# Hybrid decoder layer on one core: warm products at the start, keys copied by transfers, a sink column, and the gated output weights prepared two units earlier

## The chip, the core and the metric

The kernel runs on one core of a Trainium2 chip. A core has a matrix engine (TensorE), VectorE, ScalarE and POOL (GpSimd) for elementwise work, and SyncE (SP), whose queue issues the transfers. Every engine takes its instructions in a fixed order, from its own queue. The metric is the device time of one execution in microseconds (us). In the rows, PE is TensorE, PEld its weight load, DVE VectorE, ACT ScalarE.

## The reference, cut to what matters

One decoder layer over 2048 tokens of width 1024: a modulated norm, one input projection, two groups of heads beside each other, an output projection whose result is gated, and a final norm.

```python
mod = jnp.dot(jax.nn.silu(c), w_ada) + b_ada
shift, scale, gate = jnp.split(mod, 3, axis=-1)
h = rmsnorm(x, g_norm) * (1.0 + scale) + shift
proj = jnp.einsum('bsd,de->bse', h, w_in)
gq, gk, gv, ga, gz, sq, sk, sv, sz = split_cols(proj, COL_SIZES)
z = jnp.einsum('bsr,rk->bsk', ga, w_decay) + b_decay
o_gla = gla_chunked(gq, gk, gv, log_sigmoid(z) / 16)      # 4 heads, chunks of 64
o_gla = rmsnorm(o_gla, g_gla_head) * silu(gz)
q, k = rope(sq, positions), rope(sk, positions)           # 8 query heads, 2 key heads of 64
# window of 128; one sink logit for each head joins the softmax and is dropped after it
probs = softmax(concat([scores, sink], -1))[..., :-1]
o_swa = einsum(probs, sv) * silu(sz)
y = jnp.einsum('bse,ed->bsd', concat([o_gla, o_swa]), w_out)
x = rmsnorm(x + gate * y, g_final)
```

Everything is float32. A product that has to be exact enough is made from two parts of each operand, a rounded high part and the rest (`h` and `l` in names), with three products: high x high, low x high, high x low.

## The kernel before

The tokens are worked through in four units of 512. In each, the norm's result (`hh`, `hl`, eight pairs of tiles) is multiplied with the input weights slot by slot: `qk`, `gz`, `sz`, `gv` and `sq` twice each, `kv` once. A slot's weights are fetched into one of two buffers (`wp`); the first unit splits them and keeps the parts in memory (`wc`), the others fetch them from there. `proj_t` gives products `pt`, `proj_n` gives `pn`. In between come the heads: `gla` (one call for a pair of heads; on VectorE its chain goes from `de` through the scans `bc`, `dd` and `qk` to the transposes `pk` on TensorE), and `swa_tile` (queries transposed into `pq`, split into `qs`; scores `psc`; the softmax in `s`; `ppt`, `ppo`). `k_rows` transposes a unit's keys into `pkr` and puts their parts into `kst`, for each of two key heads a high and a low tile, in which both halves of the 128 partitions hold the same 64 rows; `pq` and `pkr` share one buffer of the matrix engine's memory (tag `pqk`). `norm(u + 1)` prepares the next unit. After the last unit, 16 calls of `out_tile` multiply the mixed heads (`mixd`) with the output weights `wo` (products `py`).

At the start, `norm0_start` sums the squares of the first unit with products `ss`, `silu_rows` spreads the conditioning vector with products `pb`, and `warm` adds products `pw` whose result nobody reads. `proj_t_outer` then makes the first six products (`po`) while their weights (`wr_first`) and the modulation (`wa`) arrive.

`late_rows` computes the gate (`wg` loads, `gate` steps on VectorE, products `pg`), multiplies each block of `w_out` with it (`wor`), and splits it. It is called in the fourth unit. The first four blocks of each half stay on the chip; the other four are written to memory (`woc`) and fetched by `last_rows`.

The order of the instructions on every engine is no plain program order. Each call is recorded with its reads and writes, and `Order.issue` simulates the engines with a table of costs and lays down the order in which the recorded calls become ready there; among calls that are ready on an engine, the one with the lowest number goes first. `od.lift` is added to that number: -LIFT (600) moves a call forward, LATER (400) back. `od.together()` keeps calls side by side. In a trace all these instructions have the lines of three helpers (L377, L424, L429), so they are told apart by their tiles.

Of the kernel before, what the change touches and what calls it, by code (L numbers as in the profile page):

```python
# [8 lines left out]
F32 = mybir.dt.float32  # L9
# [47 lines left out]
LATE_AT = 'sz0'  # L57
WO_EARLY, WO_LATE = (0, 1, 2, 3), (4, 5, 6, 7)
WARM = 13
# [323 lines left out]
def layer_kernel(ctx, tc, x, xT, w_ada, w_gate, b_cols, b_gate, g_cols, c_cols, pos, inv_freq,  # L383
# [48 lines left out]
    def warm(n, after):  # L432

        p = att.tile([P, P], F32, name="pw", tag="pqk")
        for _ in range(n):
            mmul(p, ones, ident, True, True).deps.add(after)
# [21 lines left out]
    def load_small():  # L458
# [4 lines left out]
        nsk = const.tile([P, 8], F32, name="nsk")  # L463
        V.tensor_scalar(nsk, sk, -1.0, None, op0=ALU.mult)
        return gh, sk, nsk
# [93 lines left out]
    def late_rows():  # L559

        for i in range(2):
            sl = slice(i * NB, (i + 1) * NB)
            acc = keep.tile([P, NB], F32, name=f"gate{i}", tag="r1")
            for k in range(KT):
                wg = stp.tile([P, NB], F32, name=f"wg{i}{k}", tag="xs", bufs=2)
                SY.dma_start(wg, w_gate[:, k, sl])
                if k == 0:
                    V.tensor_scalar(acc, wg, s_c[:, 0:1], None, op0=ALU.mult)
                else:
                    V.scalar_tensor_tensor(acc, wg, s_c[:, k:k + 1], acc,  # L570
                                           op0=ALU.mult, op1=ALU.add)
            parts = [stp.tile([P, NB], F32R, name=f"ga{i}{j}", tag="xs", bufs=2) for j in range(2)]
            A.copy(parts[0], acc)
            V.tensor_tensor(parts[1], acc, f(parts[0]), ALU.subtract)
            pg = att.tile([P, NB], F32, name=f"pg{i}", tag="px")
            for j in range(2):
                mmul(pg, ones_r, parts[j], j == 0, j == 1)
            bg = stp.tile([P, NB], F32, name=f"bg{i}", tag="xs", bufs=2)
            SY.dma_start(bg, b_gate[:, sl].broadcast_to([P, NB]))
            V.tensor_tensor(acc, pg, bg, ALU.add)  # L580
            for k in range(KT):
                raw = stp.tile([P, NB], F32, name=f"wor{k}{i}", tag="st")
                SY.dma_start(raw, w_out[k * P:(k + 1) * P, sl])
                V.tensor_tensor(raw, raw, acc, ALU.mult)
                if k in WO_EARLY:
                    h_ = hp.tile([P, NB], F32R, name=f"woh{k}{i}", tag="hh")
                    l_ = hp.tile([P, NB], F32R, name=f"wol{k}{i}", tag="hl")
                else:
                    h_, l_ = [stp.tile([P, NB], F32R, name=f"wo{j}{k}{i}", tag="st") for j in "xy"]
                wo[k, i] = h_, l_  # L590
                A.copy(h_, raw)
                V.tensor_tensor(l_, raw, f(h_), ALU.subtract)
                if k not in WO_EARLY:
                    for j in range(2):
                        SY.dma_start(f(woc[:, j, k, sl]), f(wo[k, i][j]))

    def last_rows():

        for k in WO_LATE:
            for i in range(2):  # L600
                wo[k, i] = [hp.tile([P, NB], F32R, name=f"wo{j}{k}{i}", tag=f"h{j}") for j in "hl"]
                for j in range(2):
                    SY.dma_start(f(wo[k, i][j]), f(woc[:, j, k, i * NB:(i + 1) * NB]))
        for i in range(2):
# [103 lines left out]
    def rsqrt(r, ms):  # L708
# [684 lines left out]
```

## Time and profile before

| | |
|---|---|
| three timed runs | 873.10, 873.64, 873.64 us; median 873.64 |
| the profiled execution | 872.5 us, span 870.8 us |
| busy in the span | TensorE 97%, weight loads 84%, VectorE 66%, ScalarE 54%, POOL 43% |
| mean granted TensorE clock | 0.994 |
| transfers | 179.9 MB, mean 207 GB/s |

The span goes from the first to the last instruction. The granted clock is the share of 2.4 GHz that TensorE was given in a stretch; its two levels are 1.2 and 2.4 GHz. An engine's idle time matters where another engine waits for it.

### The profile page before, as it was taken

What the parts mean: (1) busy time and instruction counts of PE and PEld (TensorE: products, weight loads), DVE (VectorE), ACT (ScalarE), POOL (GpSimd) and SP (SyncE); (2) the same over time, 40 slices, a digit from 0 to 9 for tenths busy, and PEclk for the clock granted to TensorE, in tenths of its full rate; (3) what the DMA queues carried; (4) which work ended last, traced back from release to release, by engine and by line L of the source; (5) the groups of instructions that cost most, each with busy time, mean ns of one, the idle gap of its engine ahead of it and who ended that gap; (6) DMA issues with size and microseconds to landing.
All of it is one profiled execution on the core that took longest, in us unless ns stands there. A gap on an engine that the chain in (4) does not pass through costs nothing. (4 is left out here: it accounts for less than half of the span.)

```text
span 870.8 us, 14663 instructions
## 1 busy us (share of the span) xinstructions
PE 841.4 (97%) x5122; PEld 732.0 (84%) x5122; DVE 578.7 (66%) x1132; ACT 470.8 (54%) x1178; POOL 374.6 (43%) x436
## 2 busy tenths in 40 slices
PE   6999989999999999999999999998999999999997
PEld 4788979789898887898897989887879888888886
DVE  4997699877575577767447786877766654444442
ACT  3677657686464577646536655464386633333332
POOL 2621346658446345744425565244337242222221
PEclk9999999999999999999999999999999999999999
DMA  8969996774443466545337564759474864444421
GB/s 340 324 255 329 352 358 227 275 276 142 152 182 116 154 238 227 204 130 195 124 116 260 191 221 162 256 204 345 147 260 158 302 193 146 145 145 145 146 73 48
DMA packets 76000, 179.90 MB, mean 207 GB/s; under 512 B 8420, under 2 KB 24855, under 8 KB 72727
## 3 DMA queue, kind: packets, MB, share of 16 engines
q1 hardware_dynamic: 74918, 178.93, 58.5%
q8 instruction: 40, 0.66, 0.3%
q14 instruction: 34, 0.27, 0.1%
q10 hardware_dynamic: 1008, 0.05, 0.1%
HBM read 134.78 MB, written 44.17 MB: 206 GB/s over the span
## 5 line engine op out<-in xcount | busy, mean ns | idle before, releaser
L424 PE MATMUL py<-woh,m 128*128 128x512 f32 (+2 forms) x528 | 160.7, 385 | 0.1
L424 PEld LDWEIGHTS py<-woh,m 128*128 128x128 f32 x528 | 98.4, 188 | 20.1 <-DVE r L377 0.5
L424 PE MATMUL py<-wol,m 128*128 128x512 f32 (+2 forms) x264 | 101.4, 384 | 0.0
L377 POOL TENSOR_TENSOR r<-r,gf 128x512 f32<-128x512 f32 x31 | 45.8, 1480 | 114.6 <-ACT xr L377 111.9
L377 ACT ACTIVATE ge<-ge 128x512 f32<-128x512 f32 x96 | 60.6, 631 | 37.4 <-DVE ge L377 36.2
L424 PE MATMUL pn<-wh_gv,hh 128*128 128x272 f32 (+1 forms) x256 | 73.7, 288 | 0.0
L424 PE MATMUL pn<-wl_sq,hh 128*128 128x256 f32 x256 | 73.5, 288 | 0.2 <-DMA wl_sq<-wc 0.2
L424 PE MATMUL pn<-wh_sq,hl 128*128 128x256 f32 x256 | 73.4, 287 | 0.0
L424 PE MATMUL pn<-wh_gv,hl 128*128 128x272 f32 (+1 forms) x256 | 73.3, 287 | 0.0
L424 PE MATMUL pn<-wl_gv,hh 128*128 128x272 f32 (+1 forms) x256 | 73.3, 287 | 0.0
L424 PE MATMUL pn<-wh_sq,hh 128*128 128x256 f32 x256 | 72.7, 286 | 0.0
L377 DVE TENSOR_TENSOR r<-py,xr 128x512 f32<-128x512 f32 (+2 forms) x33 | 22.3, 675 | 62.5 <-PE py L424 62.5
L377 ACT ACTIVATE s<-s,nm 128x128 f32<-128x128 f32 x128 | 50.1, 393 | 20.7 <-DVE nm L377 20.5
L424 PEld LDWEIGHTS py<-wol,m 128*128 128x128 f32 x264 | 49.6, 188 | 9.7
L377 POOL TENSOR_TENSOR s<-s,den 128x512 f32<-128x512 f32 x32 | 35.6, 1111 | 43.7 <-DVE den L377 31.8
L377 POOL TENSOR_TENSOR xt<-xt,rstd 128x512 f32<-128x512 f32 x27 | 38.0, 1411 | 37.2 <-ACT rstd L377 15.6
L424 PEld LDWEIGHTS pn<-wl_sq,hh 128*128 128x128 f32 x256 | 49.4, 193 | 1.5 <-DMA wl_sq<-wc 0.4
L377 POOL TENSOR_TENSOR qr<-qr,rope 128x256 f32<-128x256 f32 x32 | 27.0, 863 | 54.1 <-DVE rope L377 54.1
L424 PEld LDWEIGHTS pn<-wh_sq,hl 128*128 128x128 f32 x256 | 49.3, 193 | 1.0 <-issue 0.3
L424 PEld LDWEIGHTS pn<-wh_sq,hh 128*128 128x128 f32 x256 | 49.2, 193 | 0.8 <-issue 0.2
L424 PEld LDWEIGHTS pn<-wh_gv,hh 128*128 128x128 f32 x256 | 48.4, 189 | 0.6
L424 PEld LDWEIGHTS pn<-wl_gv,hh 128*128 128x128 f32 x256 | 48.4, 189 | 0.5
(262 smaller groups left out, 2515.9 us busy)
## 6 DMA issues: line engine op xcount, KB each, us to landing
xr<-in_x SPq DMA_DIRECT2D x32, 256.0 KB, 2.8
mr<-mixd SPq DMA_DIRECT2D x16, 512.0 KB, 4.0
out<-r SPq DMA_DIRECT2D x32, 256.0 KB, 2.3
wa<-in_w_ada SPq DMA_DIRECT2D x7, 1024.0 KB, 7.7
xn<-in_x SPq DMA_DIRECT2D x24, 256.0 KB, 4.9
xt<-in_xT SPq DMA_DIRECT2D x24, 256.0 KB, 4.5
wl_sz<-wc SPq DMA_DIRECT2D x12, 512.0 KB, 5.8
wh_sz<-wc SPq DMA_DIRECT2D x12, 512.0 KB, 6.2
```

What stands on the lines that cost most here:

```text
L377: return order.add(eng, lambda: real(*args, **kw), dur, ins, outs, lock=lock, nbytes=nbytes)
L424: return od.add("PE", lambda: T.matmul(o, l, r, start=start, stop=stop), dur, [l, r] + ([] if start else [o]), [bank if start and bank is ...
```

## The change

- `warm(WARM0, None)` puts 14 products `pw` of 128 columns ahead of everything else on TensorE; nothing reads them.
- `k_rows` writes one half of each `kst` tile (ScalarE for the high part, VectorE for the low), straight from `pkr`, and SP copies it to the other half by a transfer: four for each unit. The copy `kt`, two POOL casts and two VectorE subtractions go.
- The sink becomes a 129th column of the scores (`s1`): it takes part in the maximum, the exponential and its sum. The separate exponential `es`, its addition and `nsk` go.
- The last steps of `rsqrt`, and the sums before it in `norm`, go from VectorE to POOL (three norms).
- `late_rows` becomes `out_weights(i)`, for one half of the output columns: the first is called after slot `sq1` of the second unit, the second after `sq1` of the third, with LATER. All eight blocks of a half pass through the ring of three `st` buffers and are written to `woc`; `out_fetch` brings the first four back in the fourth unit.
- The two products of a score tile's head stay side by side.

```diff
+OUT_AT = {1: ('sq1', 0), 2: ('sq1', 1)}
-LATE_AT = 'sz0'
+WARM0, WARM = 14, 13
...
-        V.tensor_tensor(t, r, r, ALU.mult)
-        V.tensor_tensor(t, t, ms, ALU.mult)
-        V.tensor_scalar(t, t, -0.5, 1.5, op0=ALU.mult, op1=ALU.add)
-        V.tensor_tensor(r, r, t, ALU.mult)
+        G.tensor_tensor(t, r, r, ALU.mult)
+        G.tensor_tensor(t, t, ms, ALU.mult)
+        G.tensor_scalar(t, t, -0.5, 1.5, op0=ALU.mult, op1=ALU.add)
+        G.tensor_tensor(r, r, t, ALU.mult)
...
+    def out_weights(i):
...
         for k in range(KT):
-                raw = stp.tile([P, NB], F32, name=f"wor{k}{i}", tag="st")
-                SY.dma_start(raw, w_out[k * P:(k + 1) * P, sl])
-                V.tensor_tensor(raw, raw, acc, ALU.mult)
-                if k in WO_EARLY:
-                    h_ = hp.tile([P, NB], F32R, name=f"woh{k}{i}", tag="hh")
-                    l_ = hp.tile([P, NB], F32R, name=f"wol{k}{i}", tag="hl")
-                else:
-                    h_, l_ = [stp.tile([P, NB], F32R, name=f"wo{j}{k}{i}", tag="st") for j in "xy"]
+            raw, h_, l_ = [stp.tile([P, NB], dt, name=f"wo{j}{k}{i}", tag="st")
+                           for j, dt in (("r", F32), ("x", F32R), ("y", F32R))]
+            SY.dma_start(raw, w_out[k * P:(k + 1) * P, sl])
+            V.tensor_tensor(raw, raw, acc, ALU.mult)
+            A.copy(h_, raw)
+            V.tensor_tensor(l_, raw, f(h_), ALU.subtract)
+            for j, t in enumerate((h_, l_)):
+                SY.dma_start(f(woc[:, j, k, sl]), f(t))
...
-        kt = near.tile([P, NB], F32, name="kt", tag="ge", bufs=1)
-        A.copy(kt, pt)
         for kv in range(2):
-            src = half[kv]
             kh, kl = [x[:, P:] for x in kst[kv]]
-            A.copy(kh[src], kt[src])
-            G.tensor_copy(kh[half[1 - kv]], kt[src])
-            for h in half:
-                V.tensor_tensor(kl[h], kt[src], f(kh[src]), ALU.subtract)
+            A.copy(kh[half[kv]], pt[half[kv]])
+        for kv in range(2):
+            kh, kl = [x[:, P:] for x in kst[kv]]
+            V.tensor_tensor(kl[half[kv]], pt[half[kv]], f(kh[half[kv]]), ALU.subtract)
+        for kv in range(2):
+            for x in kst[kv]:
+                SY.dma_start(f(x[half[1 - kv], P:]), f(x[half[kv], P:]))
...
+        s1 = tmp.tile([P, 4, P + 1], F32, name="s", tag="s_s", bufs=2)
+        s = s1[:, :, 0:P]
+        A.copy(s1[:, :, P], sk[:, 4 * kv:4 * kv + 4])
...
-        V.scalar_tensor_tensor(nm, mx, -0.125, nsk[:, hs], op0=ALU.mult, op1=ALU.min)
-        es = tmp.tile([P, 4], F32, name="es", tag="es")
-        V.tensor_tensor(es, sk[:, hs], nm, ALU.add)
-        A.activation(es, es, AF.Exp)
+        V.tensor_scalar(nm, mx, -0.125, None, op0=ALU.mult)
...
-        V.tensor_tensor(den, den, es, ALU.add)
...
+    warm(WARM0, None)
     srow = silu_rows()
...
-        if u == NU - 1 and name == LATE_AT:
-            late_rows()
+        if u in OUT_AT and name == OUT_AT[u][0]:
+            od.lift = LATER
+            out_weights(OUT_AT[u][1])
+            od.lift = 0
+        if u == NU - 1 and name == ORDER[0]:
+            od.lift = LATER
+            out_fetch(WO_EARLY)
+            od.lift = 0
```

Since the order is laid down by a simulation, the change moves instructions that the diff does not name. Three places follow.

TensorE, the first rows of the program, as a difference from before (-) to the change (+); `ss` and `pb` as above:

```order
-L1389 UNCONDITIONAL_BRANCH
-L424 MATMUL ss<-sq_112,ones_r 128x512
+L1393 UNCONDITIONAL_BRANCH
+L424 MATMUL pw<-ident,ones_r 128x128 x14
+L424 MATMUL ss<-sq_113,ones_r 128x512
 L424 MATMUL pb<-ident_r,s_ch 128x128
 L424 MATMUL pb<-ident_r,s_cl 128x128
```

The 14 products stand alone ahead of the first `ss`; behind it nothing changed.

VectorE before, in the fourth unit, where `gla` of the first pair goes from `de` to `qk`, with the gate's second half (`gate_1248`):

```order
L377 SCALAR_TENSOR_TENSOR de<-dz 128x512
L377 TENSOR_TENSOR o<-ppo,o 64x256 x2
L377 SCALAR_TENSOR_TENSOR gate_1248<-wg_1252,s_c,gate_1248 128x512
L377 TENSOR_TENSOR pl<-ppt,ph 128x512
L377 SCALAR_TENSOR_TENSOR gate_1248<-wg_1253,s_c,gate_1248 128x512
L377 SCALAR_TENSOR_TENSOR de<-dz,de 128x512
...
L377 TENSOR_TENSOR dd<-bc 128x512
L377 SCALAR_TENSOR_TENSOR gate_1248<-wg_1254,s_c,gate_1248 128x512
L377 TENSOR_SCALAR R_1401<-Q_1006,elast,ebm 128x128
L377 SCALAR_TENSOR_TENSOR gate_1248<-wg_1255,s_c,gate_1248 128x512
...
L377 TENSOR_TENSOR qk_1374<-qk_1374,en 128x512
```

VectorE of the change, in the second unit, where `gla` of the second pair goes the same way, with the gate's first half (`gate_733`):

```order
L377 SCALAR_TENSOR_TENSOR de<-dz,de 128x512
L377 TENSOR_TENSOR pl<-ppt,ph 128x512
L377 SCALAR_TENSOR_TENSOR bc<-ones_r,de 128x128
L377 SCALAR_TENSOR_TENSOR gate_733<-wg_735,s_c,gate_733 128x512
L377 SCALAR_TENSOR_TENSOR bc<-ones_r,de 128x128
L377 RECIPROCAL den<-den 128x4
L377 SCALAR_TENSOR_TENSOR gate_733<-wg_736,s_c,gate_733 128x512
L377 SCALAR_TENSOR_TENSOR bc<-ones_r,de 128x128 x2
L377 SCALAR_TENSOR_TENSOR gate_733<-wg_737,s_c,gate_733 128x512
L377 TENSOR_TENSOR dd<-bc 128x512
...
L377 SCALAR_TENSOR_TENSOR gate_733<-wg_738,s_c,gate_733 128x512
L377 TENSOR_TENSOR qk_843<-qk_843,en 128x512
```

Four gate steps that stood in the fourth unit's chain are gone from there, and four stand in the second unit's; the gate's second half stands in the same way in the third unit's chain of the second pair. The gate's first half, before, had one step in such a chain.

SP's queue in the second unit, of the change, where the key transfers (`kst`) stand:

```order
L377 DMA wl_gv_626<-wc 128x1088 x2
L377 DMA wh_gv_625<-wc 128x1088 x2
L377 DMA mixd<-v 128x4x128
L377 DMA kst_200<-kst_200 64x512
L377 DMA kst_202<-kst_202 64x512
L377 DMA kst_201<-kst_201 64x512
L377 DMA mixd<-v 128x4x128
L377 DMA kst_203<-kst_203 64x512
L377 DMA wh_gz_631<-wc 128x1024 x2
```

They come behind the loads for slot `gv` and ahead of those for `gz`; 200 and 201 are the high and low tile of the first key head, for which the first scores wait. On TensorE the transposes `pkr` stand ahead of the scores' first product by 12 `pt`, the two of `pq` and 7 `pt` in this unit; 13 `pt` stand between `pkr` and `pq` in the first unit.

## Rows read from the trace of the kernel before

**Rows 1.** The page's first part: busy us (share of the span) and number of instructions of each engine.

```profile
PE 841.4 (97%) x5122; PEld 732.0 (84%) x5122; DVE 578.7 (66%) x1132; ACT 470.8 (54%) x1178; POOL 374.6 (43%) x436
```

**Rows 2.** Stretches of the span, from:to in us: their length, busy us (instructions) of PE, PEld, DVE, ACT and POOL, the granted clock, the DMA share and GB/s.

```profile
25.00:30.00 5.00, 3.72 (x19) 2.72 (x18) 5.00 (x6) 3.08 (x7) 4.47 (x4) 1.00 0.74 246
120.00:140.00 20.00, 18.02 (x120) 16.73 (x121) 17.27 (x42) 13.05 (x39) 6.25 (x10) 0.91 0.78 278
520.00:540.00 20.00, 20.00 (x164) 18.48 (x163) 15.02 (x27) 10.57 (x21) 10.10 (x14) 1.00 0.43 152
600.00:610.00 10.00, 7.04 (x49) 6.66 (x48) 8.09 (x14) 5.33 (x10) 1.74 (x2) 0.90 0.93 350
610.00:620.00 10.00, 10.00 (x79) 9.25 (x78) 6.57 (x10) 2.96 (x6) 5.34 (x6) 0.93 0.13 42
865.00:870.80 5.80, 0.00 (x0) 0.00 (x0) 1.44 (x5) 1.14 (x4) 0.00 (x0) 0.70 0.24 90
```

**Rows 3.** What TensorE waited for, over the whole span: us in total, times, longest.

```profile
PE pk L429 <- DVE qk L377: 2.8, 1, 2.8
...
PE gaT L429 <- ACT ga L377: 1.3, 1, 1.3
PE ppo L424 <- DVE o L377: 1.1, 2, 0.7
```

**Rows 4.** The start in order of time, POOL and TensorE: start, us, instruction, idle time before it and its releaser. A product of two float32 operands is two instructions.

```profile
1.77 0.30 POOL L377 CAST ones_r<-up_ex 128x128 fp32r<-128x128 f32 x1
...
7.57 2.05 PE L424 MATMUL ss<-sq,ones_r 128*128 128x512 f32 x2 [7.57 <-DVE s_cl L377]
...
12.30 0.41 PE L424 MATMUL pb<-ident_r,s_ch 128*128 128x128 f32 x1
12.51 0.41 PE L424 MATMUL pb<-ident_r,s_cl 128*128 128x128 f32 x1
12.73 5.13 PE L424 MATMUL ss<-sq,ones_r 128*128 128x512 f32 x6
...
13.79 0.40 POOL L377 CAST wh_first<-wr_first 128x256 fp32r<-128x256 f32 x1 [11.36 <-DMA wr_first<-in_w_in]
...
15.41 1.26 POOL L377 TENSOR_TENSOR wl_own<-wr_first,wh_own 128x512 fp32r<-128x512 f32 x1
...
17.70 3.06 PE L424 MATMUL pw<-ident,ones_r 128*128 128x128 f32 x26
...
21.39 0.35 PE L424 MATMUL po<-hh,wh_first 128*128 128x256 f32 x1 [0.63 <-ACT hh L377]
```

**Rows 5.** The first unit around its keys, TensorE and VectorE, in order of time, columns as in rows 4.

```profile
114.57 0.41 PE L429 MATMUL pq<-ident,qr 128*128 128x128 f32 x2 [0.65 <-ACT kt L377]
...
114.66 0.67 DVE L377 TENSOR_TENSOR nwt<-rr 128x4 f32<-128x4 f32 x1
115.36 1.21 DVE L377 TENSOR_TENSOR nwt<-nwt,ss 128x4 f32<-128x4 f32 x1
...
117.10 0.58 DVE L377 TENSOR_SCALAR nwt<-nwt 128x4 f32<-128x4 f32 x1
118.19 0.56 DVE L377 TENSOR_TENSOR rr<-rr,nwt 128x4 f32<-128x4 f32 x1
...
118.77 2.11 DVE L377 TENSOR_TENSOR kst<-kt,kst 64x512 fp32r<-64x512 f32 x3
...
120.91 0.42 DVE L377 TENSOR_TENSOR qs<-pq,qs 64x256 fp32r<-64x256 f32 x1
...
121.91 0.41 PE L429 MATMUL pq<-ident,qr 128*128 128x128 f32 x2 [2.15 <-DVE qs L377]
```

**Rows 6.** The fourth unit, where the gate's second half meets `gla`: VectorE and TensorE in order of time.

```profile
596.18 0.75 DVE L377 SCALAR_TENSOR_TENSOR gate<-wg,s_c,gate 128x512 f32<-128x512 f32 x1 [1.96 <-DMA wg<-in_w_gate]
...
597.98 0.92 DVE L377 SCALAR_TENSOR_TENSOR gate<-wg,s_c,gate 128x512 f32<-128x512 f32 x1 [0.33 <-DMA wg<-in_w_gate]
...
604.47 1.76 DVE L377 SCALAR_TENSOR_TENSOR gate<-wg,s_c,gate 128x512 f32<-128x512 f32 x1
...
607.71 0.88 PE L429 MATMUL pk<-ident,qk 128*128 128x128 f32 x4 [2.80 <-DVE qk L377]
```

**Rows 7.** What VectorE waited for in 560 to 700 us: us in total, times, longest.

```profile
DVE wor L377 <- DMA wor<-in_w_out: 5.7, 6, 1.9
```

**Rows 8.** Transfers by tile: queue, number, KB of each, median us from issue to landing.

```profile
mixd<-o SPq DMA_DIRECT2D x32, 128.0 KB, 3.2
...
wg<-in_w_gate SPq DMA_DIRECT2D x16, 256.0 KB, 6.4
...
wh_gv<-wc SPq DMA_DIRECT2D x6, 544.0 KB, 6.2
```

**Rows 9.** Instructions by tile: engine, operation, number: duration in ns, least/median/most.

```profile
L377 DVE TENSOR_TENSOR es<-sk,nm x32: 131/161/1218, 130.3 to 662.0; 128x4 f32<-128x4 f32 x32
...
L377 DVE TENSOR_TENSOR den<-den,es x32: 132/164/744, 136.3 to 664.0; 128x4 f32<-128x4 f32 x32
...
L377 DVE TENSOR_TENSOR kst<-kt,kst x16: 676/690/1198, 117.6 to 548.8; 64x512 fp32r<-64x512 f32 x16
...
L377 ACT CAST kst<-kt x8: 616/620/626, 114.5 to 544.9; 64x512 fp32r<-64x512 f32 x8
```

**Rows 10.** A piece of the chain that ended last: 28 products `pt` in a row, start and us.

```profile
673.47 6.37 PE pt L424 x28
```

More of the change, by code (lines that the diff above doesn't have):

```diff
@@ L435, in warm @@
         for _ in range(n):
-            mmul(p, ones, ident, True, True).deps.add(after)
+            i = mmul(p, ones, ident, True, True)
+            if after is not None:
+                i.deps.add(after)
     c_sb = const.tile([P, KT], F32, name="c_sb")
@@ L462, in load_small @@
         A.dma_start(sk, sinks.broadcast_to([P, 8]))
-        nsk = const.tile([P, 8], F32, name="nsk")
-        V.tensor_scalar(nsk, sk, -1.0, None, op0=ALU.mult)
-        return gh, sk, nsk
+        V.tensor_scalar(sk, sk, 8.0, None, op0=ALU.mult)
+        return gh, sk
     pf = const.tile([P, 16], F32, name="pos_f")
@@ L557, in layer_kernel @@
     gfin = []
[L559 to L568, printed above, removed]
-                else:
[L570 to L581, printed above, removed]
-                raw = stp.tile([P, NB], F32, name=f"wor{k}{i}", tag="st")
-                SY.dma_start(raw, w_out[k * P:(k + 1) * P, sl])
-                V.tensor_tensor(raw, raw, acc, ALU.mult)
-                if k in WO_EARLY:
-                    h_ = hp.tile([P, NB], F32R, name=f"woh{k}{i}", tag="hh")
-                    l_ = hp.tile([P, NB], F32R, name=f"wol{k}{i}", tag="hl")
-                else:
-                    h_, l_ = [stp.tile([P, NB], F32R, name=f"wo{j}{k}{i}", tag="st") for j in "xy"]
[L590 to L595, printed above, removed]
@@ L597, in last_rows @@
-    def last_rows():
-        for k in WO_LATE:
+    def out_weights(i):
+        sl = slice(i * NB, (i + 1) * NB)
+        acc = keep.tile([P, NB], F32, name=f"gate{i}", tag="r1")
+        for k in range(KT):
+            wg = stp.tile([P, NB], F32, name=f"wg{i}{k}", tag="xs", bufs=2)
+            SY.dma_start(wg, w_gate[:, k, sl])
+            if k == 0:
+                V.tensor_scalar(acc, wg, s_c[:, 0:1], None, op0=ALU.mult)
+            else:
+                V.scalar_tensor_tensor(acc, wg, s_c[:, k:k + 1], acc, op0=ALU.mult, op1=ALU.add)
+        parts = [stp.tile([P, NB], F32R, name=f"ga{i}{j}", tag="xs", bufs=2) for j in range(2)]
+        A.copy(parts[0], acc)
+        V.tensor_tensor(parts[1], acc, f(parts[0]), ALU.subtract)
+        pg = att.tile([P, NB], F32, name=f"pg{i}", tag="px")
+        for j in range(2):
+            mmul(pg, ones_r, parts[j], j == 0, j == 1)
+        bg = stp.tile([P, NB], F32, name=f"bg{i}", tag="xs", bufs=2)
+        SY.dma_start(bg, b_gate[:, sl].broadcast_to([P, NB]))
+        V.tensor_tensor(acc, pg, bg, ALU.add)
+        for k in range(KT):
+            raw, h_, l_ = [stp.tile([P, NB], dt, name=f"wo{j}{k}{i}", tag="st")
[6 more added lines that the diff above has]
+                SY.dma_start(f(woc[:, j, k, sl]), f(t))
@@ L600, in last_rows, with out_fetch @@
+    def out_fetch(ks):
+        for k in ks:
             for i in range(2):
@@ L603, in last_rows @@
                     SY.dma_start(f(wo[k, i][j]), f(woc[:, j, k, i * NB:(i + 1) * NB]))
+    def last_rows():
+        out_fetch(WO_LATE)
         for i in range(2):
@@ L1043, in sink @@
             for i in range(2):
+                vs[tt + i] = v[:, i]
+            for i in range(2):
                 kr[tt + i] = kt[:, i]
-                vs[tt + i] = v[:, i]
         return sink
@@ L1110, in swa_tile @@
                 dst = ps[:, h2, 2 * P - nj:]
-                mmul(dst, qs[:, h], kh[:, j0:j0 + nj], True, False)
-                mmul(dst, qs[:, h], kl[:, j0:j0 + nj], False, True)
+                with od.together():
+                    mmul(dst, qs[:, h], kh[:, j0:j0 + nj], True, False)
+                    mmul(dst, qs[:, h], kl[:, j0:j0 + nj], False, True)
             sp = s[:, 2 * pr:2 * pr + 2]
@@ L1251, in layer_kernel @@
     V.tensor_tensor(b1, b1, g_sb, ALU.mult)
-    gh, sk, nsk = load_small()
+    gh, sk = load_small()
     wk, w_load, w_part, w_keep = first_w()
```

11 lines of the change are left out of this document (4 added, 7 removed).

## The prediction

> **What bounds the kernel now.** I first read the page's busy shares: TensorE is busy 841.4 of the 870.8 us [rows 1], so 29.4 us is all the idle time there is to win, plus what TensorE loses while it runs at half clock. The change takes no product away (it adds 14 small ones at the start), so the question is only which of TensorE's waits go and which come. Next I read its waits [rows 3], then the stages around them. There are four places:
>
> - The start: the first product comes at 7.57 us, and the stream of products that lasts begins at 21.39 [rows 4].
> - The first unit: waits of 0.65 and 2.15 us at 114.57 and 121.91 [rows 5]. In 120 to 140 the granted clock is 0.91 [rows 2], so 0.09 x 20 = 1.8 us of the full 2.4 GHz is lost.
> - The fourth unit, 587 to 608 us: 2.8 us for VectorE's `qk`, 1.3 for `gaT`, 0.7 for `o` [rows 3, 6]; the clock then shows 0.90 and 0.93 over two stretches of 10 us [rows 2], which loses 1.0 + 0.7 = 1.7 us.
> - The end: 5.8 us without TensorE work [rows 2], which the change does not touch.
>
> The rest is small waits. In between TensorE is full: 20.00 of 20 us in 520 to 540 [rows 2].
>
> **The start.** Until 17.70 the engine runs at the lower level, 1.2 GHz. The granted clock is not recorded there, so I go by durations: six `ss` instructions of 512 columns take 5.13 us, 0.855 each, while 26 `pw` instructions of 128 columns take 3.06 us from 17.70, 0.118 each, or 0.47 for 512 columns; `pb` comes at steps of 0.21 us before [rows 4]. TensorE had then been working for 10.1 us, since 7.57.
>
> The change puts 14 `pw` products (28 instructions) ahead. `ones_r` is ready at 1.77 + 0.30 = 2.07 [rows 4]. At the low clock they take 28 x 2 x 0.118 = 6.6 us, to 8.7. Eight `ss` instructions and 16 `pb` follow: at full clock 8 x 0.43 + 16 x 0.11 = 5.2 us, at the low one twice that. Before, the last `ss` ended at 12.73 + 5.13 = 17.86.
>
> - Clock up when the 14 end: last `ss` at 8.7 + 5.2 = 13.9, a gain of 4.0 us. Up earlier: the 14 end sooner, but the first `ss` has its data only at 7.57, as now, so 12.8 and a gain of 5.1 at most.
> - Clock up as long after the first product as before, 10.1 us, at 12.2: by then two `ss` instructions (1.7) and 9 `pb` are done; the rest takes 3.4, to 15.6: a gain of 2.3.
>
> I take 4.2 and keep 2.3 to 5.1. Does it reach the first `po`? That comes 3.5 us after the last `ss` (17.86 to 21.39) [rows 4], through ScalarE and VectorE, so at about 17.2; the first weights land at 13.79 and POOL has split them at 15.41 + 1.26 = 16.7 [rows 4]. Behind it VectorE is busy 5.00 of 5 us in 25 to 30 while the DMA share falls to 0.74 [rows 2]: VectorE's chain sets the pace there, not the transfers, and it moves with the start.
>
> **Keys and the first unit.** `k_rows` loses its ScalarE copy `kt`, two POOL casts and two of four VectorE subtractions; four transfers fill the other halves. In the first unit VectorE was late: between 114.66 and 120.91 it ran four tiny operations of the norm in 0.67 + 1.21 + 0.58 + 0.56 = 3.0 us, and three of the four `kst` subtractions in 2.11 [rows 5]. The norm's go to POOL, which is busy only 6.25 of 20 us in 120 to 140 [rows 2] and where the multiplication by `rstd` queues behind them, for a unit that starts 40 us later; two of the four `kst` go, 0.69 each [rows 9]. That is 3.0 + 1.4 = 4.4 us less ahead of the `qs` for which TensorE waited 2.15. So these waits and the clock loss go: 0.65 + 2.15 + 1.8 = 4.6 us.
>
> What comes instead: `pq` now needs the buffer that both subtractions read, and the unit's `pt` products queue behind it on TensorE. From `pkr` the buffer takes 0.62 (ScalarE) + 0.69 + 0.69 (VectorE) = 2.0 us [rows 9]; 13 `pt` lie between, 13 x 0.2275 = 3.0 us [rows 10]. So it is covered by 1 us, which a late VectorE uses up. I charge 1.5 us: net -3.1, bounds -4.6 and 0.
>
> In the second unit the first scores come 12 + 7 `pt` = 4.3 us after `pkr`. The halves need 0.62 + 0.69, the third issue at SP (about 1.7 us after `pkr`), and the landing; at SP the weights of `gz` queue behind them, which TensorE needs a slot later. No row shows a transfer within the chip's memory. The nearest is `mixd<-o`, of the same 128 KB, 3.2 us; a 544 KB weight load, which stands just ahead in SP's queue, takes 6.2 [rows 8]. So they land at 4.9 to 7.9: a wait of 0.6 to 3.6 us, or none if such a transfer is quicker. I take 1.0, as the size is that of the first; bounds 0 and 3.6 + 1.8 of clock = 5.4. In the third and fourth unit over 11 us of products stand between, so nothing. The Trainium skill (DMA: Bandwidth & Descriptors, Latency and other measured facts) says that most of a transfer's fixed cost is the receipt from the target memory, and HBM is the slowest; by it a transfer that ends in SBUF lands sooner than `mixd<-o`, this 1.0 is 0 and the sum 1 us lower. No run here shows one yet.
>
> **The sink column.** Two VectorE operations of 0.161 and 0.164 us leave each of 32 tiles [rows 9], 10.4 us in all, and ScalarE's small exponential becomes a small copy. Neither engine is the bound, so I count nothing; it is slack for the waits above.
>
> **The output weights.** The fourth unit loses the gate and the split. What they cost there [rows 6]: VectorE waited 1.96 + 0.33 us for `wg` and spent 0.75 + 0.92 + 1.76 us in three gate steps, all ahead of the `qk` for which TensorE waited 2.80 at 607.71. With `gaT` and `o` next to it and the clock that is 2.8 + 1.3 + 0.7 + 1.7 = 6.5 us saved.
>
> But the same work now stands in the second and third unit. The order shows the point: before, the first half had one gate step inside GLA's chain from `de` to `qk` on VectorE, and cost TensorE nothing (520 to 540: 20.00 of 20 [rows 2]); the second half had four there, and that is the wait above. After, both halves have four there, and behind a late `wg` the whole chain queues, for which TensorE's `pk` waits. Bounds: 0, as the first half, and 2 x 6.5 = 13.0, as the second twice. For the high end: the same queue, and `wg` takes 6.4 us to land [rows 8]. Against it: in the new places fewer loads of `w_out` compete, and VectorE has less other work. I take 5.0. The 32 added transfers of 256 KB are hidden behind the units' products; uncovered, the last would cost one landing, 6 us, but the early fetch has the whole fourth unit.
>
> **Sum.** -4.2 - 3.1 + 1.0 - 6.5 + 5.0 = -7.8 us. The profiled execution took 872.5 us (span 870.8), so 864.7; the timed median is 873.64, 1.1 above it, which gives **865.8 us**. A measurement of this kernel tells about 0.2% (1.7 us) from no change.
>
> **The rivals.**
> - *As above*, 862 to 870: 0.48.
> - *The new waits do not come* (output weights 0, keys 0, first unit clean, start at its best): -5.1 - 4.6 - 6.5 = -16.2, 857.4. For it: the first half cost nothing before. 0.17.
> - *Both gate halves stall TensorE in full*: 13.0 in place of 5.0, so +0.2: 873.8. For it: four gate steps in each chain. 0.15, a third each below, within and above 0.2%.
> - *Slower: VectorE's queue stands behind the moved loads.* Every `w_out` block now goes through the ring of three `st` buffers, where before half of them did; VectorE waited 5.7 us in six waits for `wor`, 0.95 each [rows 7]. For 34 loads that is 32 us; if half of it reaches TensorE, with two clock losses, 16 + 3.5 = 19.5 in place of 5.0: +6.7, 880.3. It decides from 12.8 us, 0.38 us a load. Against it: the six waits fell where TensorE lost little. 0.10.
> - *The change does not do what it says at the start*: the clock stays low, and the 28 instructions hold the first `ss` until 8.7: 1.1 us late in place of 4.2 early, 871.1. 0.10.
>
> **How the numbers follow.** Faster: 0.48 + 0.17 + 0.05 + 0.08 of the last = 0.78; within 0.2%: 0.05 + 0.02 = 0.07; slower: 0.15. The range goes from the second case to the third and leaves out the slower rival: 857 to 874.
>
> **What would show it.** After: `pw` from about 2.1 us, `ss` at 0.43 an instruction, the last near 13.7 and the first `po` near 17; no wait over 1.5 us at the first unit's `pq`; no clock below 1.00 near 600 us. Wrong, if `ss` still takes 0.855, if TensorE waits at `pk` in the second or third unit for over 2 us each, or at `psc` for `kst`, with the clock falling behind it.

## The result and the profile after

| kernel | median us | runs | ratio to before | 95% interval |
|---|---|---|---|---|
| before | 875.17 | 15 | | |
| changed | 870.32 | 15 | 0.9946 | 0.9930 to 0.9961 |

The changed kernel is 0.54% faster, 4.7 us. The forecast was -7.8 us: the sign is right, the size too large by two thirds. The twelve runs of the kernel before that were timed beside the changed one lie a little higher (873.8 to 876.9) than the three shown earlier. The two profiled executions happen to stand closer together than the medians (spans of 870.8 and 869.9 us), so I compare them place by place and take sizes from the timed runs. One execution also differs from the next in its falls of the clock: the mean granted clock of the fifteen runs goes from 0.990 to 0.998.

The page of the changed kernel, busy time of each engine, beside [rows 1]:

```profile
PE 842.0 (97%) x5150; PEld 735.2 (85%) x5150; DVE 557.1 (64%) x1042; ACT 472.6 (54%) x1174; POOL 366.3 (42%) x446
```

VectorE lost 90 instructions and 21.6 us of work; TensorE's idle time is 27.9 us in place of 29.4. At the start alone 7.57 us became 2.11, filled with the 14 products that nobody reads, so behind the start the idle time rose by 4 us. What TensorE waited for, over the whole span (us in total, times, longest), beside [rows 3]:

```profile
PE psc L424 <- DMA kst<-kst: 3.8, 3, 2.4
PE po L424 <- ACT hh L377: 2.3, 2, 1.5
...
PE pk L429 <- DVE pl L377: 1.9, 2, 1.5
PE pq L429 <- POOL ss L377: 1.7, 1, 1.7
```

The 2.8 us of `pk` for `qk` and the 1.3 of `gaT` are gone. New on top stands a wait that the forecast priced at nothing after the second unit: scores that wait for the transferred half of the keys.

The start of the changed kernel, TensorE in order of time, beside [rows 4]:

```profile
2.11 5.69 PE L424 MATMUL pw<-ident,ones_r 128*128 128x128 f32 x28 [2.11 <-POOL ones_r L377]
...
10.24 2.79 PE L424 MATMUL ss<-sq,ones_r 128*128 128x512 f32 x6
...
16.79 0.36 PE L424 MATMUL po<-hh,wh_first 128*128 128x256 f32 x1 [0.86 <-ACT hh L377]
...
23.98 0.77 PE L424 MATMUL po<-hh,wh_first 128*128 128x512 f32 x1 [1.46 <-ACT hh L377]
```

VectorE behind it, first before, then in the changed kernel:

```profile
20.05 1.21 DVE L377 SCALAR_TENSOR_TENSOR wa<-wa,pb 128x1024 f32<-128x1024 f32 x1
...
23.32 1.29 DVE L377 TENSOR_TENSOR hl<-xt,hh 128x256 fp32r<-128x256 f32 x2
```
```profile
16.25 1.22 DVE L377 SCALAR_TENSOR_TENSOR wa<-wa,pb 128x1024 f32<-128x1024 f32 x1 [0.73 <-DMA wa<-in_w_ada]
...
19.04 2.45 DVE L377 TENSOR_TENSOR hl<-xt,hh 128x256 fp32r<-128x256 f32 x2
```

The first unit around its keys, TensorE, beside [rows 5]:

```profile
113.84 0.41 PE L429 MATMUL pq<-ident,qr 128*128 128x128 f32 x2 [0.18 <-DVE kst L377]
...
121.96 0.41 PE L429 MATMUL pq<-ident,qr 128*128 128x128 f32 x2 [1.06 <-DVE qs L377]
```

Stretches of the changed kernel, columns as in [rows 2]:

```profile
15.00:30.00 15.00, 12.01 (x64) 10.07 (x63) 14.27 (x18) 8.79 (x19) 11.27 (x11) 0.89 1.02 412
120.00:140.00 20.00, 17.65 (x131) 16.35 (x131) 17.89 (x30) 14.65 (x41) 10.85 (x14) 1.00 0.85 314
400.00:410.00 10.00, 7.62 (x44) 7.17 (x43) 3.36 (x7) 3.15 (x8) 0.53 (x2) 0.83 1.04 361
600.00:610.00 10.00, 9.68 (x61) 8.58 (x61) 7.04 (x13) 4.88 (x12) 5.05 (x7) 1.00 0.61 203
```

The falls of the clock at 120 to 140 and at 600 are gone, and two others have come: one in the ada phase, behind the 1.46 us wait at 23.98, and one at 400 to 410, behind the longest wait for the keys. Each of these falls took 3.41 us at the lower level, so about 1.7 us.

Where the moved work runs, in time: the multiplication of the `w_out` blocks with the gate, before, and in the changed kernel in the third unit and in the fourth (whose first product starts at 511.3 us).

```profile
L377 DVE TENSOR_TENSOR wor<-wor,gate x16: 679/691/998, 551.4 to 651.6; 128x512 f32<-128x512 f32 x16
```
```profile
L377 DVE TENSOR_TENSOR wor<-wor,gate x8: 682/693/1047, 367.1 to 429.8; 128x512 f32<-128x512 f32 x8
```
```profile
L377 DVE TENSOR_TENSOR wor<-wor,gate x8: 661/692/1119, 544.2 to 603.3; 128x512 f32<-128x512 f32 x8
```

The calls stand behind the second and the third unit's `sq1`, but, put back by LATER, most of their work runs a unit later. So only the first half left the fourth unit, for the third; the second half's split still stands in the fourth. The forecast had both halves leave it.

Finally the third unit of the changed kernel, which gives back most. SP's queue, then ScalarE, VectorE and TensorE, in order of time:

```profile
377.64 8.63 SPq L377 DMA_DIRECT2D xn<-in_x  x3
...
389.06 1.24 SPq L377 DMA_DIRECT2D kst<-kst  x2
...
398.78 0.47 SPq L377 DMA_DIRECT2D kst<-kst  x1
```
```profile
384.54 0.69 DVE L377 TENSOR_TENSOR wor<-wor,gate 128x512 f32<-128x512 f32 x1 [2.02 <-DMA wor<-in_w_out]
...
385.19 0.63 ACT L377 ACTIVATE xn<-xn 128x512 f32<-128x512 f32 x1 [3.11 <-DMA xn<-in_x]
...
387.48 1.17 ACT L377 CAST kst<-pkr 64x512 fp32r<-64x512 f32 x2
...
388.68 1.39 DVE L377 TENSOR_TENSOR kst<-pkr,kst 64x512 fp32r<-64x512 f32 x2 [0.93 <-ACT kst L377]
...
390.21 0.41 PE L429 MATMUL pq<-ident,qr 128*128 128x128 f32 x2 [1.66 <-POOL ss L377]
...
405.98 1.60 PE L424 MATMUL psc<-kst,qs 128*128 128x256 f32 x7 [2.38 <-DMA kst<-kst]
```

Three in-order queues stand in turn: SP's for 8.6 us at three loads of `xn`, ScalarE's for 3.1 us at one of these loads, with the copy of the keys (`kst`) behind it, VectorE's at a `w_out` block that has not landed and then at that copy. The wait of 1.66 us at `pq` is put down to the norm's `ss` on POOL, which had ended at 389.9 us. But `pq` shares its buffer with `pkr`, and VectorE's subtractions read `pkr` until 390.07; `pq` starts 0.14 us behind them, as it does in the first unit (113.70 to 113.84). So this wait belongs to the keys. The four key transfers go out in two pairs 10 us apart, and the scores wait for the last. VectorE's waits over the span; of before those for `wor` were 5.7 us in six [rows 7]:

```profile
DVE wor L377 <- DMA wor<-in_w_out: 17.9, 8, 5.9
DVE woy L377 <- ACT wox L377: 5.9, 7, 1.2
```

### The profile page after: what moved, and what is told of

Read it like the earlier page. It is cut to its first block, busy times and chain, and to the rows that moved or that the text cites. A ratio compares the mean times of both kernels' runs of the same rounds, so it can differ in the third digit from the quotient of the medians.

```text
span 869.9 us, 14694 instructions
## 1 busy us (share of the span) xinstructions
PE 842.0 (97%) x5150; PEld 735.2 (85%) x5150; DVE 557.1 (64%) x1042; ACT 472.6 (54%) x1174; POOL 366.3 (42%) x446
## 4 chain that ended last, share of the span: by engine, by line
PE 66%; DMA 14%; DVE 10%; ACT 6%; issue 3%; POOL 1%; SPq 1%; ACTq 0%; DVEq 0%; POOLq 0%
PE py L424 20%; PE pn L424 17%; PE pt L424 13%; PE po L424 6%; PE psc L424 3%; PE ppo L424 3%; DMA xn<-in_x 2%; DMA kst<-kst 2%; DMA wg<-in_w_gate 2%; PE ppt L429 1%; DMA bg<-in_b_gate 1%; DVE ge L377 1%; DMA wc<-wl_qk 1%; DMA wa<-in_w_ada 1%; DMA xt<-in_xT 1%
## 5 line engine op out<-in xcount | busy, mean ns | idle before, releaser
L377 ACT ACTIVATE s<-s,nm 128x129 f32<-128x129 f32 x128 | 51.0, 400 | 15.3 <-DVE nm L377 14.1
L424 PE MATMUL psc<-kst,qs 128*128 128x256 f32 (+1 forms) x256 | 43.9, 292 | 7.7 <-DMA kst<-kst 3.8
L377 POOL TENSOR_TENSOR o<-o,zs 128x128 f32<-128x128 f32 x64 | 36.9, 596 | 33.4 <-DVE o L377 33.0
```

Source lines behind the costliest of these rows:

```text
L377: return order.add(eng, lambda: real(*args, **kw), dur, ins, outs, lock=lock, nbytes=nbytes)
L424: return od.add("PE", lambda: T.matmul(o, l, r, start=start, stop=stop), dur, [l, r] + ([] if start else [o]), [bank if start and bank is ...
```

## The experiments

My theory after these traces: the start and the fourth unit gained about what was forecast, and the transferred keys, late in the third and fourth unit, gave back 5 us. Its rival: the moved output weights gave it back. The first four kernels undo one part of the change each; they, and every later kernel, were timed beside the kernel before on the same chip. The changed kernel was not timed again, so I set a kernel against it by the two ratios to before, and put the difference in us into the last column (of 874 us). From the two intervals such a difference is sure to 1.9 to 2.4 us.

| kernel | median us | before beside it | ratio | 95% interval | against changed, us |
|---|---|---|---|---|---|
| keys_back | 878.48 | 874.52 | 1.0047 | 1.0029 to 1.0064 | +8.8 |
| norm_back | 867.69 | 874.52 | 0.9935 | 0.9913 to 0.9957 | -1.0 |
| no_warm | 873.03 | 874.52 | 0.9989 | 0.9973 to 1.0005 | +3.8 |
| out_back | 867.78 | 874.52 | 0.9933 | 0.9914 to 0.9952 | -1.1 |
| only_keys | 870.93 | 874.23 | 0.9967 | 0.9950 to 0.9983 | +1.8 |
| only_early | 869.86 | 874.23 | 0.9960 | 0.9944 to 0.9977 | +1.2 |
| only_out | 877.01 | 874.23 | 1.0031 | 1.0014 to 1.0048 | +7.4 |
| out_norm_back | 864.81 | 874.23 | 0.9896 | 0.9873 to 0.9919 | -4.4 |
| own_ring | 869.15 | 874.20 | 0.9950 | 0.9931 to 0.9969 | +0.3 |
| stores_act | 870.49 | 874.20 | 0.9970 | 0.9952 to 0.9988 | +2.1 |
| early_sink | 870.71 | 874.20 | 0.9963 | 0.9944 to 0.9982 | +1.5 |
| mult_pool | 868.26 | 874.49 | 0.9944 | 0.9923 to 0.9965 | -0.2 |

### One part undone

**keys_back**: `k_rows` as before the change.

```diff
+        A.copy(kt, pt)
...
-            A.copy(kh[half[kv]], pt[half[kv]])
...
-                SY.dma_start(f(x[half[1 - kv], P:]), f(x[half[kv], P:]))
+            A.copy(kh[src], kt[src])
+            G.tensor_copy(kh[half[1 - kv]], kt[src])
+            for h in half:
+                V.tensor_tensor(kl[h], kt[src], f(kh[src]), ALU.subtract)
```

> The changed kernel with the key rows made the old way again (a copy `kt`, GpSimd's copies and four subtractions, no transfers between halves); the early products, the moved output weights, the sink column and the norm on GpSimd stay. Theory (the key transfers gave back part of the gain: TensorE waited 2.4 us for `kst` in the third unit, where the clock then fell for 1.7 us, and 1.5 us in the fourth; against that the first unit's 2.1 us wait for VectorE's queue comes back): 2 to 4 us faster than the changed kernel, 7 to 9 us faster than the kernel before, no wait of `psc` for a transfer left. Rival (the moved output weights and GpSimd's norm gave it back, the transfers are nearly free): as the changed kernel or up to 3 us slower than it, 2 to 5 us faster than before.

8.8 us slower than the changed kernel: the theory falls at once, and so does the rival's size. The profiled execution is the slowest of its nine (881.1 us), so its waits may be longer than in the others. No score waits for a transfer any more, but VectorE and ScalarE are late instead. VectorE ran the four subtractions in one piece, where the changed kernel has two of 0.69, and in the second unit ScalarE's queue was late with `ph`:

```profile
113.59 4.11 DVE L377 TENSOR_TENSOR kst<-kt,kst 64x512 fp32r<-64x512 f32 x4
...
190.97 0.66 PE L424 MATMUL ppo<-ph,vs 128*128 128x512 f32 x1 [3.14 <-ACT ph L377]
```

The clock fell there too. I put that second wait down to the planner, which laid the whole unit out anew; if so, the 8.8 us are not the price of the key rows by themselves.

**norm_back**: the six operations of the norm on VectorE again.

```diff
-        G.tensor_tensor(t, r, r, ALU.mult)
...
+        V.tensor_tensor(t, r, r, ALU.mult)
...
-        G.tensor_tensor(ss, sq[:, :, 0], sq[:, :, 1], ALU.add)
...
+        V.tensor_tensor(ss, sq[:, :, 0], sq[:, :, 1], ALU.add)
```

> The changed kernel with the six small operations of the norm (ss, rr) on VectorE again. Theory (on GpSimd they stand in order before a rope step on which `pq` waited 1.66 us in the third unit): that wait goes, 1 to 2 us faster than the changed kernel. Rival (VectorE beside the moved output weights is the shorter-handed engine): the same as the changed kernel or up to 2 us slower, with the longer waits now on VectorE.

The medians, taken at different times, differ by 2.6 us; by the ratios it is 1.0, which cannot be told from no change, so theory and rival stay undecided. The wait of 1.66 us at `pq` shrank to half, and what is left is now put down to VectorE's subtractions, again 0.14 us ahead:

```profile
385.50 1.39 DVE L377 TENSOR_TENSOR kst<-pkr,kst 64x512 fp32r<-64x512 f32 x2 [0.93 <-ACT kst L377]
```
```profile
387.03 0.41 PE L429 MATMUL pq<-ident,qr 128*128 128x128 f32 x2 [0.83 <-DVE kst L377]
```

TensorE's idle time in 345 to 515 us did not fall (6.18 for 6.02). What fell is 60 to 175 us, the changed kernel first, then norm_back:

```profile
60.00:175.00 115.00, 110.14 (x762) 99.26 (x762) 91.11 (x167) 79.55 (x190) 48.60 (x61) 1.00 0.87 309
```
```profile
60.00:175.00 115.00, 112.29 (x774) 100.72 (x773) 92.97 (x176) 81.64 (x196) 49.99 (x58) 1.00 0.89 318
```

2.15 us less idle in the first unit, though VectorE has nine instructions more there. In 515 to 685 us, where no norm runs, it is 2.1 us less too (1.66 for 3.79), so some of the difference is only a new order.

**no_warm**: no early products.

```diff
-WARM0, WARM = 14, 13
+WARM0, WARM = 0, 13
```

> The changed kernel without the 14 early products. Theory (the start brings 4.6 us to the first ada product but half is given back before the phase ends, through VectorE, the w_ada transfers and a second fall of the clock): 2.0 to 2.5 us slower than the changed kernel. Rival (all of the start reaches the end): 4 to 5 us slower. Second rival (the phase is set by transfers): no difference.

3.8 us slower by the ratios, 2.7 by the medians, which does not tell the theory from the first rival. The first product of the ada phase comes 4.4 us later (21.22), and its last starts 2.2 us later (56.23 for 54.04). Part of the start's gain is given back inside the phase.

**out_back**: both halves of w_out times gate in the fourth unit, as before the change.

```diff
-        if u in OUT_AT and name == OUT_AT[u][0]:
-            od.lift = LATER
-            out_weights(OUT_AT[u][1])
...
+        if u == NU - 1 and name == LATE_AT:
+            late_rows()
```

> The changed kernel with both halves of w_out times gate in the fourth unit again. Theory (the move took 4.8 us of waits and a fall of the clock of 1.7 us out of the fourth unit and cost 1.5 to 2.5 us in the second and third): 3 to 5 us slower than the changed kernel; SP's queue in the third unit is emptier then, and the wait of `psc` for the transferred keys shorter. Rival (the move cost as much as it brought, 5 us of new work beside VectorE): within 1.5 us of the changed kernel.

The theory, 3 to 5 us slower, falls: it is 1.1 us faster by the ratios (2.5 by the medians), within the noise, as the rival has it. The move brings nothing here. In the third unit SP issues the four key transfers from 377.97 us in one run, and TensorE waits for none of them in any unit:

```profile
377.97 2.51 SPq L377 DMA_DIRECT2D kst<-kst  x4
```

So in the changed kernel the late keys were a consequence of the moved work, not a property of the transfers.

### One part alone, and the best pair

**only_keys**, **only_early**, **only_out**: the kernel before with one part each: the new `k_rows`, the early products, or `out_weights` and `out_fetch` at their new places. The first and the last also hold the two products of a score tile's head together.

```diff
only_keys
-                V.tensor_tensor(kl[h], kt[src], f(kh[src]), ALU.subtract)
...
+                SY.dma_start(f(x[half[1 - kv], P:]), f(x[half[kv], P:]))
only_early
+    warm(WARM0, None)
only_out
-            late_rows()
...
+            out_weights(OUT_AT[u][1])
...
+            out_fetch(WO_EARLY)
```

> The kernel before with one part of the change alone, the key rows by transfers (with the psc pairs held together, as in the changed kernel). After undoing the parts one by one, theory: the key rows carry most of the gain, since putting the old ones back cost 8 us; 3 to 6 us faster than before, through VectorE's and GpSimd's shorter queues at the start of each unit's attention (two subtractions instead of four, no GpSimd copies). Rival (in the old order the transfers land late and give it back; the 8 us came from how the old key rows fit the rest of the changed kernel): within 1.5 us of before.

> The kernel before with one part alone, the 14 early products. Theory (half of the start is given back inside the ada phase): 2.0 to 3.5 us faster than before. Rival (all of it reaches the end): 4 to 5 us faster. Second rival (it only moves the falls of the clock): within 1 us.

> The kernel before with one part alone, w_out times gate moved into the second and third unit, all of it kept in memory and fetched by the last (psc pairs held together). Theory (the move pays in new stalls what it saves in the fourth unit, and 10.5 MB more of transfers stand in SP's queue): from no change to 3 us slower than before. Rival (the forecast's terms, -6.5 in the fourth unit and +5.0 at most in the others): 1.5 to 4 us faster than before.

Against before, keys -3.3 us by the medians (0.33%, 2.9 us, by the ratio), early products -4.4 (0.40%, 3.5 us), output weights +2.8 (0.31%, 2.7 us): each is clear of the noise. The last, where the idle time lies: 175 to 345, 345 to 515 and 515 to 685 us, the kernel before, then only_out.

```profile
175.00:345.00 170.00, 168.81 (x1105) 149.93 (x1105) 116.22 (x247) 107.64 (x293) 88.79 (x110) 1.00 0.53 182
345.00:515.00 170.00, 168.67 (x1102) 148.67 (x1101) 111.46 (x231) 96.93 (x257) 86.09 (x109) 1.00 0.53 186
515.00:685.00 170.00, 164.70 (x1093) 144.55 (x1092) 125.55 (x239) 94.51 (x243) 77.00 (x95) 0.99 0.64 219
```
```profile
175.00:345.00 170.00, 168.16 (x1099) 148.74 (x1099) 118.14 (x245) 105.13 (x286) 91.12 (x116) 1.00 0.51 179
345.00:515.00 170.00, 163.41 (x1070) 143.66 (x1069) 124.53 (x249) 100.63 (x261) 83.57 (x98) 1.00 0.67 229
515.00:685.00 170.00, 167.06 (x1094) 147.79 (x1093) 109.25 (x222) 93.22 (x238) 75.37 (x99) 1.00 0.65 224
```

Idle time of TensorE: 1.19 to 1.84, 1.33 to 6.59 and 5.30 to 2.94 us. The fourth unit gives 2.4 us (and 1.7 of the clock), the third takes 5.3. VectorE is busy 13.1 us more in the third unit, but it does not stand at the loads there; its waits for them, only_out, third unit and fourth:

```profile
DVE wor L377 <- DMA wor<-in_w_out: 2.1, 2, 1.7
```
```profile
DVE wor L377 <- DMA wor<-in_w_out: 10.2, 6, 3.1
```

So TensorE loses 5.3 us where VectorE waits 2.1 for `wor`, and gains where it waits 10.2.

**out_norm_back**: the edits of out_back and norm_back together; what stays of the change is the early products, the key transfers and the sink column.

> The changed kernel with two parts undone together: w_out times gate back in the fourth unit and the norm's six small operations back on VectorE; what stays is the early products, the key transfers and the sink column. Theory (each alone gained 2.5 us on the changed kernel, at different places): 864 to 866 us, 4 to 6 us faster than the changed kernel. Rival (they gain the same thing, VectorE's or GpSimd's room in the third unit): 867 to 869 us, as each alone.

864.81 us, by the ratios 4.4 less than the changed kernel: together the two are clear of the noise. With the other one undone, each is worth something too: the output weights 3.4 us (against norm_back, sure to 2.8), the norm 3.2 (against out_back, sure to 2.6). This is the best version here, 1.0% faster than before. Its idle time in the third unit is back at 1.81 us, and the gate in the fourth unit, with all its eight steps per half, keeps `pk` waiting for 0.9 us at most, where it was 2.8:

```profile
345.00:515.00 170.00, 168.19 (x1097) 149.01 (x1096) 108.04 (x211) 93.64 (x240) 79.43 (x98) 1.00 0.53 186
```
```profile
PE pk L429 <- DVE qk L377: 1.1, 2, 0.9
```

**early_sink**: the kernel before with the early products and the sink column.

```diff
-        V.tensor_reduce(mx, s, AX.X, ALU.max)
+        V.tensor_reduce(mx, s1, AX.X, ALU.max)
...
+    warm(WARM0, None)
```

> The kernel before with two parts of the change, the early products and the sink column (with the psc pairs held together); the key rows, w_out times gate and the norm as before. The early products alone gave 3.5 us. Theory (the sink column takes three small operations of VectorE and one of ScalarE out of each attention tile and adds one copy, which is worth little beside the stalls): 3 to 5 us faster than before, so 0 to 1.5 us for the sink column, and 4 to 6 us for the key rows as the difference to the kernel that has early products, keys and sink column (864.8 us). Rival (the sink column is what keeps the attention tiles' chain short): 6 us or more faster than before.

870.71 us, against 869.86 for the early products alone: the sink column gives nothing that can be measured. The keys, as the step from here to 864.81, give 5.9 us in this company, as expected, and 3.3 alone. Where they give it, 60 to 175 and 515 to 685 us of early_sink, then of out_norm_back:

```profile
60.00:175.00 115.00, 109.21 (x756) 99.42 (x755) 91.62 (x168) 76.56 (x183) 50.08 (x54) 0.99 0.88 311
...
515.00:685.00 170.00, 162.53 (x1078) 142.88 (x1079) 123.68 (x224) 91.77 (x233) 70.38 (x89) 1.00 0.66 225
```
```profile
60.00:175.00 115.00, 111.76 (x769) 100.12 (x768) 92.08 (x176) 81.49 (x193) 49.60 (x56) 1.00 0.91 327
...
515.00:685.00 170.00, 167.01 (x1131) 146.88 (x1130) 117.14 (x223) 94.41 (x239) 68.74 (x92) 1.00 0.70 236
```

Idle time falls from 5.79 to 3.24 us in the first unit and from 7.47 to 2.99 in the fourth; in the second and third it rises, by 1.1 and 0.4.

### What the moved output weights cost in the third unit

Three kernels take away one named wait each.

**own_ring**: the tiles `wg`, `ga` and `bg` share no buffers with the norm's loads.

```diff
-            wg = stp.tile([P, NB], F32, name=f"wg{i}{k}", tag="xs", bufs=2)
+            wg = stp.tile([P, NB], F32, name=f"wg{i}{k}", tag="st")
```

> The changed kernel with the gate's tiles (wg, ga, bg) in the ring of three buffers that the split itself uses (`st`), no longer in the ring of two (`xs`) that the norm's loads `xn` need. Theory (the move costs its time in the third unit through what it delays: the gate holds the two `xs` buffers, so the `xn` loads come some 33 us later than with the split in the fourth unit, stand in SP's queue with the stores of the split, and the key rows and their transfers come 10 us late): the key rows are split earlier than 387 us, the 2.4 us wait of `psc` for `kst` in the third unit shrinks or goes, with it the fall of the clock there, and the kernel is 1.5 to 4 us faster than the changed one. Rival (the cost is the work and the stores themselves, wherever the gate's buffers lie): within 1 us of the changed kernel.

The mechanism is as expected and the gain is not there. The key transfers go out together from 384.4 us, no score waits for them, and the clock does not fall in that unit; the time is 869.15, which cannot be told from the changed kernel. Idle time in 345 to 515 us is 6.92. VectorE now stands at the same loads earlier, in the chain of the linear attention:

```profile
369.49 0.69 DVE L377 TENSOR_TENSOR wor<-wor,gate 128x512 f32<-128x512 f32 x1 [3.86 <-DMA wor<-in_w_out]
...
373.26 0.27 DVE L377 TENSOR_TENSOR Q<-R,pu 128x128 f32<-128x128 f32 x1
```
```profile
373.68 1.13 PE L424 MATMUL po<-sT,v 128*128 128x128 f32 x8 [2.90 <-DVE Q L377]
```

**stores_act**: the stores to `woc` from ScalarE's queue.

```diff
-                SY.dma_start(f(woc[:, j, k, sl]), f(t))
+                A.dma_start(f(woc[:, j, k, sl]), f(t))
```

> The changed kernel with the 32 stores of the split output weights issued from ScalarE's queue in place of SP's. Theory (SP's queue stands behind stores that wait for the split, and the key transfers behind them): the key transfers of the third unit no longer come in two pairs 10 us apart, and the kernel is 1 to 3 us faster than the changed one. Rival (the loads `xn` and the buffers are what SP waits for, or ScalarE now stands where SP stood): the same as the changed kernel or up to 3 us slower.

No gain (870.49; the profiled execution, 874.2, is the slowest of its twelve): the four key transfers are closer together (399.8 to 403.1) but all late, and `pms` waits 2.6 us for VectorE's `osq`, `pk` 2.5 for its `pl`. The rival holds.

**mult_pool**: norm_back, and the product with the gate on GpSimd.

```diff
-            V.tensor_tensor(raw, raw, acc, ALU.mult)
+            G.tensor_tensor(raw, raw, acc, ALU.mult)
```

> The changed kernel with the norm back on VectorE (867.7 us by itself) and, besides, the 16 products of a w_out block with the gate (wor<-wor,gate) on GpSimd in place of VectorE. In the changed kernel VectorE stood 17.9 us at those 16, waiting for the load, with the unit's chain queued behind it. Theory (that standing in VectorE's in-order queue is what the moved output weights cost): 864.5 to 866.5 us, VectorE's waits for wor gone, TensorE idle in 345 to 515 us down from 6.2 to 3 to 4. Rival (GpSimd then stands there, with the rope steps and the norm's product behind it, or the cost is in ScalarE's and SP's queues): 867 to 870 us, idle there still 5 us or more.

The rival again: 868.26, idle 6.48 us in 345 to 515. GpSimd stands at the loads instead, and VectorE one step further on, at ScalarE's cast:

```profile
POOL wor L377 <- DMA wor<-in_w_out: 30.5, 10, 8.9
```
```profile
DVE woy L377 <- ACT wox L377: 17.0, 8, 6.9
```

So three named causes were taken away in turn, and the time stayed. In 345 to 515 us TensorE is idle for 4.6 to 7.3 us in every kernel with the moved work in it, and for 0.8 to 3.4 in every one without; its removal brought back 5.3 us (only_out to before), 4.4 (norm_back to out_norm_back) and 2.9 (to out_back). That the moved work costs this is shown. Which part of it does is not: no run moved the gate without the split, and beside standing at loads VectorE simply has 8 to 13 us more to do there. What would make it harmless in that place is open; a larger ring of buffers for it was not tried.

## Why the prediction was right or wrong, point by point

- **The sum.** -7.8 forecast, -4.7 measured. It was right in sign because the two large gains are real; two of its terms had the wrong sign and partly hid behind a third that was too small. That the sum came out nearer than its terms is luck. One of the signs of being wrong came: scores waited for `kst`, 2.38 us at 405.98, and the clock fell behind it.
- **The start, -4.2.** The mechanism held: `ss` takes 0.465 us an instruction, the last ends at 13.03 for 17.86, and the first `po` comes 4.60 us earlier. At the end 3.5 (only_early) to 3.8 us (no_warm) are left by the ratios, 4.4 and 2.7 by the medians. Within the ada phase it did not all hold: VectorE's chain did not move "with the start". Its first `wa` there came 3.8 us earlier, after 0.73 us of waiting for the transfer, its two `hl` took 2.45 us for 1.29, and TensorE waited 1.46 at 23.98. VectorE is busy 14.27 of the 15 us from 15 to 30, at a DMA share of 1.02; which of the two sets the pace now is not shown. The fall of the clock behind that wait is not needed for it: in only_early the same wait of 1.47 us stands at 24.21, the clock did not fall, and the last product of the phase starts at 53.52, 2.9 us earlier than before (56.39).
- **Keys and the first unit, -3.1.** The waits of 0.65 and 2.15 us became 0.18 and 1.06, and the clock stays up; the buffer that `pq` needs cost 0.18, not 1.5. The key rows are worth 3.3 us alone, 5.9 with the early products and the sink column. The forecast charged the first unit alone; of the idle time that went in that company, 2.6 us lie in the first unit and 4.5 in the fourth, while the second and third lost 1.5.
- **The norm on GpSimd.** This is the step that failed in that term. I took its four small operations (3.0 us) as a pure relief of VectorE, since POOL was busy only 6.25 of 20 us. With the output weights in the fourth unit it costs 3.2 us (out_back against out_norm_back); in the changed kernel itself the cost, 1.0, is within the noise (norm_back). In both pairs TensorE's idle time in the first unit is 2.2 us shorter with the norm on VectorE (4.86 to 2.71 and 5.45 to 3.24). POOL's busy share did not tell that; which wait carries the cost is not shown, and the 1.66 us at the third unit's `pq` is not it. With the key rows shortened the relief was no longer there: in the first unit of norm_back the four take 0.48, 0.15, 0.17 and 0.16 us on VectorE.
- **Keys in the later units, +1.0 and nothing.** In the second unit no wait came, in the third and fourth 2.4 and 1.5 us, and one fall of the clock. I had looked at the products between the transposes and the scores, 11 us, and not at what stands ahead of the transfers on SP. Without the moved work (out_back, out_norm_back) no score waited for a transfer. The Trainium skill (DMA: Bandwidth & Descriptors, Latency and other measured facts), by which a transfer that ends in SBUF lands sooner than one to HBM, is not what these rows show: `kst<-kst` lands in 4.4 us in the median, 2.3 to 7.0, and `mixd<-o` of the same 128 KB, which goes to HBM, in 3.0. Why is open: the two were issued beside different loads of the queues.
- **The output weights, -6.5 and +5.0.** Measured +2.8 alone, 3.4 with the norm on VectorE, and 1.1, within the noise, in the changed kernel. The step that failed stands in its first sentence, "the fourth unit loses the gate and the split": in time only the first half left, and the second half's split still runs there, from 544 to 603 us. So the -6.5 was too large, the fourth unit gave 4.1; and one half in the third unit cost as much as I had charged for both (5.3, and 0.65 in the second; only_out). It was not the way that I named: the gate's steps ahead of `pk` stand beside waits of 0.4 and 1.5 us, without a fall of the clock. Nor is it my slower rival, at a chance of 0.10, as I worked it out. VectorE's waits for `wor` did rise from 5.7 to 17.9 us, but 7.1 of these lie in the fourth unit, and in only_out the third unit loses 5.3 us with 2.1 of them. And it was no fixed price of the gate there, since with the keys and the early products in, `pk` waits 0.9 us and the clock stays up.
- **The sink column, 0.** Right, as far as can be told (early_sink).

## What to carry to other kernels

Before a chain of load, compute and store is moved into another stage's queues, ask of each in-order queue what will stand behind each of its steps and waits there; an engine's free share in that stage did not answer it here. Where a planner lays down the order, look at when the moved work runs, not at where it is called. A stall that several causes make together is not the price of any one of them: three cures of one wait each brought nothing here. When a change has several parts, time them alone and undone; here two of five cost 4.4 us between them, and the sum still looked like a success.

## What the runs showed of the hardware

- By the clock that the two traces record, it rose to 2.4 GHz at 6.97 us in the changed kernel, 4.9 us after the first product, and at 17.4 in the kernel before, 9.9 us after its first; TensorE showed no idle time between in either. Waits of the same length did not always end in a fall: behind 1.46 us at 23.98 it fell in one kernel and behind 1.47 at 24.21 in another it did not.
- Transfers between two halves of SBUF partitions (64 by 512, 128 KB) landed after 2.3 to 7.0 us in the changed kernel, and one issue at SP took 0.46 to 1.2 us.
